# Gate and up stage of an encoder: who casts, who sums and who empties PSUM

## The chip, the core and the metric

One core of one Trainium2 chip runs the whole kernel in one launch. TensorE (PE; PEld is its weight load) multiplies, VectorE (DVE), ScalarE (ACT) and GpSimd (POOL) do the rest, and SyncE (SP) issues the DMAs. The metric is the device time of one execution in microseconds; lower is better. Three runs of the kernel before took 3045.6 to 3051.87 us, median 3049.84.

## The reference, cut to what matters

Two encoder layers over 1024 tokens of width 1024, in float32. Each layer has a mixer (attention), a layer norm, a gated feed-forward with a convolution of width 3 over the tokens, another layer norm, and a gated addition of an embedding. The change lies in the first half of the feed-forward, in both layers:

```python
def conv_ffn(x, w_gate, w_up, conv_w, conv_b, w_down):   # x 1024x1024, w_gate and w_up 1024x2816
    a = x @ w_gate
    u = x @ w_up
    ap = jnp.pad(a, ((0, 0), (pad, pad), (0, 0)))
    c = conv_b
    for j in range(CONV_WIDTH):
        c = c + conv_w[j] * ap[:, j:j + S]
    return (jax.nn.gelu(c) * u) @ w_down
```

## The kernel before

**How the work is staged.** A layer runs as projections and attention, output projection and layer norm, the gate and up stage, the down projection, and the embedding. The gate and up stage takes x transposed, with the even and the odd tokens apart, and cuts `w_gate` and `w_up` into 22 pieces (`NF`), gate and up by turns: piece m holds two blocks of 128 output columns. Each piece is one matrix product of 2 x 2 blocks, done by the Strassen-Winograd scheme with seven block products in place of eight. The weights' sides of the seven are `a00`, `a01`, `a11` (blocks as loaded) and the sums `s1` to `s4`; the sides of x are `b00`, `b10`, `b11` and `t1` to `t4`, made once in the layer (in the trace `xb` and `xt`).

**Float32 by three matmuls.** TensorE multiplies values of a shorter format (float32r). So each operand is split: a cast gives its high part, a subtraction on VectorE the low part (`lo_part`, line 142), and `mm3` (lines 159 to 161) issues high x high, high x low and low x high. A block product is 4 x 3 = 12 matmuls of 512 columns, added up in one PSUM bank.

**The helpers that the change touches.** `Weights.sums` makes `s1` to `s4`: with an engine given, `s1`'s first addition and `s3` run there and the other two on VectorE (`ws` in the trace, line 319). `Weights.split` casts one side and subtracts: for the names in `HI` (`s3`, `a01`, `a11`) the cast is GpSimd's (`pool_copy`, line 139), for the other four ScalarE's (line 325). `Weights.steps` lists the sums and the seven splits of a piece.

`Products.read` empties PSUM and adds the products up to the four result blocks, as far as they are there: `m` is ScalarE's copy of the product `a00`; `u2 = m + s2`, `u3 = u2 + s3` and so on are additions on VectorE with one operand in PSUM (`plus`, line 1332). The products `a00` and `s2` of a piece share one tile of two banks (`pa`, two such tiles); the other five rotate through four banks (`pb`). The first two pieces go ahead (`go_ahead`): their products come in another order, `s1` before `s2`, with an extra copy of `s1` (`k5`) that two additions then use (lines 1353 and 1354).

**What sets the order.** The tile framework puts each engine's instructions into a fixed order when the program is built, by its own estimate of when each can run, and adds the waits; on the chip an engine works through its order and stops at a wait. The list `order` in `ffn` gives the products: the first two pieces interleaved, then seven products for each of the rest. The third piece's preparation (`todo`) is spread over the first two pieces' last products, and each later piece's over the products of the one before.

Of the kernel before, what the change touches and what calls it, by code (L numbers as in the profile page):

```python
# [12 lines left out]
ALU = mybir.AluOpType  # L13
# [19 lines left out]
def tile_hybrid_encoder(  # L33
# [32 lines left out]
    nc = tc.nc  # L66
# [12 lines left out]
    def unit(s, shape, dt=F32):  # L79
        return up.tile(shape, dt, tag="u", name=nm(s))  # L80
# [26 lines left out]
    def rtile(s, shape, dt=F32R):  # L107
        return region[0].tile(s, shape, dt)
# [7 lines left out]
    def mid2(s, shape, dt=F32):  # L116
        return sm.tile(shape, dt, tag="mid2", name=nm(s), bufs=4)
# [10 lines left out]
    def f32(ap):  # L128
        return ap.bitcast(F32)
# [8 lines left out]
    def pool_copy(o, i):  # L138
        nc.gpsimd.tensor_scalar(o, i, 1.0, 1.0, op0=ALU.mult, op1=ALU.mult)  # L139

    def lo_part(lo, src, hi):
        nc.vector.tensor_tensor(lo, src, f32(hi), op=ALU.subtract)  # L142

    def split(raw, h, l, hi=None, lo=None):
        if hi is nc.scalar:
            nc.scalar.copy(h, raw)  # L146
        else:
            pool_copy(h, raw)
        (lo or nc.vector).tensor_tensor(l, raw, f32(h), op=ALU.subtract)  # L149

    def load_split(dram, shape, s, make=runit, hi=None, lo=None):
        r = region[0].raw(s + "r", shape)
        nc.sync.dma_start(out=r, in_=dram)
        h, l = make(s + "h", shape), make(s + "l", shape)
        split(r, h, l, hi, lo)
        return h, l
# [161 lines left out]
    def add(o, a, b, op=ALU.add, eng=None):  # L318
        return (eng or nc.vector).tensor_tensor(f32(o), f32(a), f32(b), op=op)

    def split_value(v, h, l, hi=None):
        if hi is nc.gpsimd:
            pool_copy(h, v)
        else:
            nc.scalar.copy(h, v)  # L325
        lo_part(l, v, h)
# [316 lines left out]
    class BlockB:  # L643
# [7 lines left out]
        def steps(self):  # L651
            out = []
            if self.pr % 2 == 0:
                out += [self.g.load] + [lambda t=t: self.g.project(t) for t in range(NT)]
            out.append(self.load)
            out += [lambda t=t: self.project(t) for t in range(NT)]
            return out
# [249 lines left out]
    class MixTiles:  # L907
# [4 lines left out]
        def seven(self, t):  # L912

            mr = region[0].raw("mr", [P, NK, P])
            nc.sync.dma_start(out=mr[:, 0:7, :], in_=mix[self.i].rearrange("k p q -> p k q")[:, 0:7, t * P:(t + 1) * P])
            two = [runit("mhl", [P, 2, 4, P]) for _ in range(2)]
            for j, m in enumerate(two):
                n = 4 - j
                split(mr[:, 4 * j:4 * j + n], m[:, 0, 0:n], m[:, 1, 0:n])
            self.m[t] = mr, two  # L920
# [342 lines left out]
    class Weights:  # L1263
# [22 lines left out]
            for step in steps:  # L1286
                step()

        HI = {"s3", "a01", "a11"}

        def split(self, name, raw=None):
            raw = name in ("a00", "a01") if raw is None else raw
            hl = region[0].raw("w", [P, 2, 4, P], F32R) if raw else rtile("w", [P, 2, 4, P])
            self.h[name], self.l[name] = hl[:, 0], hl[:, 1]
            split_value(self.v[name], hl[:, 0], hl[:, 1], nc.gpsimd if name in self.HI else None)

        def steps(self):

            return [lambda: self.sums(nc.gpsimd)] + [lambda n=n: self.split(n) for n in Products.ORDER]

    class Products:

# [26 lines left out]
        def read(self):  # L1329

            def plus(o, a, name):
                nc.vector.tensor_tensor(o, a, self.o[name], op=ALU.add)  # L1332
            out = []
            had = set(x for x, _ in self.sums)
            for name, need in list(self.sums):
                before = {"m": (), "u2": ("m",), "u3": ("u2",), "c11": ("u3",), "c00": ("m",) if self.ahead else ("u2",), "c10": ("u3", "c11"), "k5": (),
                          "c01": ("c11",)}[name]
                if any(x not in self.o for x in need) or any(x in had for x in before):
                    continue
                if name == "m":  # L1340
                    self.m = mid2("m", [P, 512])
                    nc.scalar.copy(self.m, self.o["a00"])
                elif name == "u2":
                    u = unit("u", [P, 2, 512])
                    self.u2, self.u3 = u[:, 0, :], u[:, 1, :]
                    plus(self.u2, self.m, "s2")
                elif name == "u3":
                    plus(self.u3, self.u2, "s3")
                elif name == "k5":
                    self.c11 = mid2("c11", [P, 512])  # L1350
                    nc.scalar.copy(self.c11, self.o["s1"])
                elif name == "c11" and self.ahead:
                    nc.gpsimd.tensor_tensor(self.u2, self.u2, self.c11, op=ALU.add)
                    nc.vector.tensor_tensor(self.c11, self.u3, self.c11, op=ALU.add)
                elif name == "c11":
                    self.c11 = mid2("c11", [P, 512])
                    plus(self.c11, self.u3, "s1")
                    plus(self.u2, self.u2, "s1")
                elif name == "c00":
                    if self.c00 is None:  # L1360
                        self.c00 = self.m
                    plus(self.c00, self.m, "a01")
                elif name == "c10":
                    plus(self.u3, self.u3, "a11")
                    self.c10 = self.u3
                elif name == "c01":
                    plus(self.u2, self.u2, "s4")
                    self.c01 = self.u2
                had.discard(name)
                out.append(name)  # L1370
            self.sums = [x for x in self.sums if x[0] in had]
            return out
# [14 lines left out]
    def ffn(i, w, xt, late, prefetch):  # L1387
# [3 lines left out]
        def new_c():  # L1391
            late_c.append(big("c", [P, 2, 1024]))
# [51 lines left out]
        def finished(n):  # L1444
            if n >= 0:
                m = order[n][0]
                for name in pr[m].read():
                    use(pr[m], m, name)
# [12 lines left out]
        todo = []  # L1461
        for n, (m, name) in enumerate(order):
            finished(n - 1)
            pr[m].product(name)
            if n == 0:
                c00 = unit("c00", [P, 2, 512])
                for a in range(2):
                    pr[a].go_ahead(c00[:, a])
                for a in range(2):
                    sums[a] = w[a].sums()  # L1470
                    sums[a][0]()
                    w[a].split("s1")
            if n == 1:
                late()
                new_c()
                temps = [late_c[0][:, a, :].rearrange("p (k q) -> p k q", k=2) for a in range(2)]
            if n == 2:
                for a in range(2):
                    sums[a][1]()
                    sums[a][2]()  # L1480
                    w[a].split("s4")
            if n == 3:
                for a in range(2):
                    xt.finish("t2", a)
                for a in range(2):
                    w[a].split("s2", True)
            if n == 4:
                for a in range(2):
                    xt.finish("t3", a)
                for a in range(2):  # L1490
                    sums[a][3]()
                    w[a].split("s3")
            if n == 5:
                for a in range(2):
                    xt.finish("t4", a, temps[a])
            if n == 6:
                w[0].split("a11")
                w[1].split("a11")
                w[2].load()
            if n == 7:  # L1500
                w[3].load()
                todo = w[2].steps()
            for _ in range({8: 1, 10: 2, 11: 1, 12: 1, 13: 3}.get(n, 0)):
                todo.pop(0)()
            if m >= 2 and m + 1 < NF:
                j = Products.ORDER.index(name)
                if j == 0:
                    todo = w[m + 1].steps()
                    todo[0]()
                    if m + 2 < NF:  # L1510
                        w[m + 2].load()
                todo[j + 1]()
            if m == NF - 1:
                down.ahead(Products.ORDER.index(name))
# [98 lines left out]
    for i in range(2):  # L1613
        if i == 0:
            w, mt, oT = mixer_ab(xt)
        else:
            tc.keep_in_program_order(nc.scalar.preload_act_table_set("natural_log_exp_and_others"))
            w, mt, oT = mixer_c(xt, late)
# [107 lines left out]
```

## Time and profile before

| | us |
|---|---|
| median of three runs | 3049.84 |
| the profiled execution | 3047.42 |
| its span in the trace | 3045.1 |
| TensorE busy | 2949.2 (97%) |
| VectorE busy | 2308.2 (76%) |
| ScalarE busy | 1318.1 (43%) |
| GpSimd busy | 963.6 (32%) |

The first layer's gate and up stage lies between about 795 and 1240 us of the span, the second layer's between about 2285 and 2730. A timeline row gives the start, the duration, engine and line, what is written from what, and in brackets how long the engine had been idle and what ended that. `xN` on a row means N equal instructions in a row, whose duration is that of all. In a row of windows the granted clock is TensorE's, as a share of full speed.

### The profile page before, as it was taken

The page shows a single profiled execution, that of the slowest core. Times are in us where ns is not written, and L with a number is a line of the kernel's source. Part 1 is how long each engine was busy: PE and PEld are TensorE (multiplying, and loading weights), DVE is VectorE, ACT ScalarE, POOL GpSimd, SP SyncE. Part 2 cuts the span into 40 slices and gives each one's busy share as a digit, 9 for nine tenths or more (in the row PEclk, how much of TensorE's full clock was granted, in tenths as well). Part 3 has the DMA queues.
Part 4 walks back from the last instruction along what each step waited for, and adds up shares of the span by engine and source line. Part 5 has one row for each costly group of instructions (what it writes and reads, how often), then busy time and mean ns, then how long its engine had stood idle before and what let it go on. Part 6 is the DMA issues. An engine that isn't in the chain of part 4 may idle for free.

```text
span 3045.1 us, 42940 instructions
## 1 busy us (share of the span) xinstructions
PE 2949.2 (97%) x15456; PEld 2533.8 (83%) x15456; DVE 2308.2 (76%) x4022; ACT 1318.1 (43%) x2806; POOL 963.6 (32%) x1484
## 2 busy tenths in 40 slices
PE   8999999999989999999999999999998999999999
PEld 7888989887768888888888999998776788888887
DVE  6666477876898888688648777777769888877874
ACT  4555477761222222345225555555413222234431
POOL 4444544243232222000225555554332222210012
PEclk9999999999999999999999999999999999999999
DMA  3000100034223332734111100001431333346331
GB/s 123 29 28 19 38 29 8 8 130 134 90 98 104 104 104 100 276 133 169 63 59 34 34 32 29 28 18 56 155 129 69 115 104 104 104 163 244 115 127 66
DMA packets 119715, 272.10 MB, mean 89 GB/s; under 512 B 11344, under 2 KB 35024, under 8 KB 119504
## 3 DMA queue, kind: packets, MB, share of 16 engines
q1 hardware_dynamic: 119504, 269.37, 26.0%
q8 instruction: 122, 2.00, 0.3%
q14 instruction: 89, 0.73, 0.1%
HBM read 196.46 MB, written 72.88 MB: 88 GB/s over the span
## 4 chain that ended last, share of the span: by engine, by line
PE 74%; DVE 15%; ACT 3%; issue 3%; POOL 3%; DMA 2%; SPq 0%; DVEq 0%; ACTq 0%; POOLq 0%
PE pb L159 5%; PE pb L161 5%; PE pb L160 5%; PE xt L164 5%; PE pp L159 4%; PE s L588 4%; PE pp L161 4%; PE pp L160 4%; PE pd L159 4%; PE pd L161 4%; PE pd L160 4%; PE pa L159 2%; PE pg L159 2%; PE pg L161 2%; PE pg L160 2%
## 5 line engine op out<-in xcount | busy, mean ns | idle before, releaser
L142 DVE TENSOR_TENSOR ptl<-xt,pth 128x512 fp32r<-128x512 f32 (+2 forms) x384 | 239.7, 652 | 60.2 <-ACT pth L399 43.6
L159 PE MATMUL pp<-wh,xth 128*128 128x384 f32 x768 | 266.1, 347 | 8.0 <-ACT wh L146 7.6
L160 PE MATMUL pp<-wl,xth 128*128 128x384 f32 x768 | 258.8, 337 | 2.0 <-DVE wl L149 1.8
L161 PE MATMUL pp<-wh,xtl 128*128 128x384 f32 x768 | 257.9, 336 | 0.0
L440 ACT ACTIVATE e<-s,nmx 128x1024 f32<-128x1024 f32 x192 | 214.7, 1120 | 81.7 <-DVE nmx L838 59.0
L160 PE MATMUL pd<-wd,gd 128*128 128x512 f32 x616 | 239.9, 389 | 0.2 <-DVE wd L142 0.2
L159 PE MATMUL pd<-wd,gd 128*128 128x512 f32 x616 | 239.8, 389 | 0.0
L161 PE MATMUL pd<-wd,gd 128*128 128x512 f32 x616 | 239.7, 389 | 0.0
L325 ACT CAST w<-ws 128x512 fp32r<-128x512 f32 x132 | 81.1, 621 | 336.6 <-PE pb L161 281.0
L164 PE MATMUL xt<-ident,e 128*128 128x128 f32 x1440 | 198.1, 274 | 9.6 <-POOL e L740 3.0
L159 PE MATMUL pb<-xt,w 128*128 128x512 f32 x528 | 207.1, 392 | 0.0
L160 PE MATMUL pb<-xt,w 128*128 128x512 f32 x528 | 206.9, 392 | 0.0
L161 PE MATMUL pb<-xt,w 128*128 128x512 f32 x528 | 206.6, 391 | 0.0
L1149 ACT CAST gd<-gr 128x512 fp32r<-128x512 f32 x154 | 96.0, 623 | 214.9 <-PE pd L161 176.1
L164 PEld LDWEIGHTS xt<-ident,e 128*128 128x128 f32 x1440 | 163.5, 141 | 30.4 <-ACT sq L870 5.9
L896 POOL TENSOR_SCALAR rs<-mv 128x1 f32<-128x1 f32 x32 | 9.3, 291 | 547.7 <-DVE mv L895 547.1
L139 POOL TENSOR_SCALAR w<-ws 128x512 fp32r<-128x512 f32 x44 | 33.4, 760 | 467.0 <-PE pa L161 416.8
L142 DVE TENSOR_TENSOR gd<-gr,gd 128x512 fp32r<-128x512 f32 x154 | 106.1, 689 | 77.1 <-ACT gd L1149 77.1
L142 DVE TENSOR_TENSOR w<-ws,w 128x512 fp32r<-128x512 f32 x176 | 152.4, 870 | 5.2 <-ACT w L325 3.1
L159 PEld LDWEIGHTS pp<-wh,xth 128*128 128x128 f32 x768 | 144.6, 188 | 13.3 <-ACT wh L146 8.2
L838 DVE TENSOR_REDUCE nmx<-s 128x1 f32<-128x1024 f32 x128 | 150.4, 1214 | 2.6 <-PE s L588 2.6
L159 PE MATMUL pb<-xb,w 128*128 128x512 f32 x352 | 139.9, 397 | 9.8 <-DVE u L1332 5.7
(292 smaller groups left out, 8905.2 us busy)
## 6 DMA issues: line engine op xcount, KB each, us to landing
gr<-gated SPq DMA_DIRECT2D x76, 512.0 KB, 3.7
gated<-c SPq DMA_DIRECT2D x90, 256.0 KB, 3.5
wf<-in_w_gate_dram SPq DMA_DIRECT2D x44, 512.0 KB, 4.1
wf<-in_w_up_dram SPq DMA_DIRECT2D x44, 512.0 KB, 4.2
wd<-in_w_down_dram SPq DMA_DIRECT2D x44, 512.0 KB, 5.5
wr<-in_w_c_dram SPq DMA_DIRECT2D x32, 384.0 KB, 3.3
gated<-u SPq DMA_DIRECT2D x44, 256.0 KB, 2.2
pes<-peo SPq DMA_DIRECT2D x64, 128.0 KB, 1.9
```

The costliest lines, as they stand in the source:

```text
L139: nc.gpsimd.tensor_scalar(o, i, 1.0, 1.0, op0=ALU.mult, op1=ALU.mult)
L142: nc.vector.tensor_tensor(lo, src, f32(hi), op=ALU.subtract)
L159: nc.tensor.matmul(o, lhsT=lh, rhs=rh, start=start, stop=False)
L160: nc.tensor.matmul(o, lhsT=lh, rhs=rl, start=False, stop=False)
L161: nc.tensor.matmul(o, lhsT=ll, rhs=rh, start=False, stop=stop)
L164: nc.tensor.transpose(o, in_=i, identity=ident)
L325: nc.scalar.copy(h, v)
L440: nc.scalar.activation(dst, s, AF.Exp, bias=negmax, scale=1.0, accum_out=l)
L588: nc.tensor.matmul(s[:, kh * 512:kh * 512 + 512], lhsT=qt[:, hl, i, :], rhs=self.ks[kh][:, j, :], start=hl == 0, stop=hl == 1)
L838: nc.vector.tensor_reduce(out=nmx, in_=s, axis=AX.X, op=ALU.max, negate=True)
L896: nc.gpsimd.tensor_scalar(rs, mv[:, 1:2], 1.0, LN_EPS, op0=ALU.mult, op1=ALU.add)
L1149: nc.scalar.copy(g[:, 0], rg)
```

## The change

In the gate and up stage of both layers: the casts of `s3`, `a01` and `a11` go from GpSimd to ScalarE, as those of the other four sides; the sums of the third and fourth piece run on VectorE alone (those of the first two did already; from the fifth piece on GpSimd keeps its two); the first two pieces' `s2` is copied out of PSUM by ScalarE, and an addition of two SBUF operands on VectorE adds `m`; and the addition of `u2` and `c11` in these two pieces goes from GpSimd to VectorE.

```diff
--- before.py
+++ after.py
@@ -1286,17 +1286,15 @@
             for step in steps:
                 step()
 
-        HI = {"s3", "a01", "a11"}
-
         def split(self, name, raw=None):
             raw = name in ("a00", "a01") if raw is None else raw
             hl = region[0].raw("w", [P, 2, 4, P], F32R) if raw else rtile("w", [P, 2, 4, P])
             self.h[name], self.l[name] = hl[:, 0], hl[:, 1]
-            split_value(self.v[name], hl[:, 0], hl[:, 1], nc.gpsimd if name in self.HI else None)
-
-        def steps(self):
-
-            return [lambda: self.sums(nc.gpsimd)] + [lambda n=n: self.split(n) for n in Products.ORDER]
+            split_value(self.v[name], hl[:, 0], hl[:, 1])
+
+        def steps(self, eng):
+
+            return [lambda: self.sums(eng)] + [lambda n=n: self.split(n) for n in Products.ORDER]
 
     class Products:
 
@@ -1343,14 +1341,18 @@
                 elif name == "u2":
                     u = unit("u", [P, 2, 512])
                     self.u2, self.u3 = u[:, 0, :], u[:, 1, :]
-                    plus(self.u2, self.m, "s2")
+                    if self.ahead:
+                        nc.scalar.copy(self.u2, self.o["s2"])
+                        add(self.u2, self.u2, self.m)
+                    else:
+                        plus(self.u2, self.m, "s2")
                 elif name == "u3":
                     plus(self.u3, self.u2, "s3")
                 elif name == "k5":
                     self.c11 = mid2("c11", [P, 512])
                     nc.scalar.copy(self.c11, self.o["s1"])
                 elif name == "c11" and self.ahead:
-                    nc.gpsimd.tensor_tensor(self.u2, self.u2, self.c11, op=ALU.add)
+                    nc.vector.tensor_tensor(self.u2, self.u2, self.c11, op=ALU.add)
                     nc.vector.tensor_tensor(self.c11, self.u3, self.c11, op=ALU.add)
                 elif name == "c11":
                     self.c11 = mid2("c11", [P, 512])
@@ -1499,13 +1501,13 @@
                 w[2].load()
             if n == 7:
                 w[3].load()
-                todo = w[2].steps()
+                todo = w[2].steps(nc.vector)
             for _ in range({8: 1, 10: 2, 11: 1, 12: 1, 13: 3}.get(n, 0)):
                 todo.pop(0)()
             if m >= 2 and m + 1 < NF:
                 j = Products.ORDER.index(name)
                 if j == 0:
-                    todo = w[m + 1].steps()
+                    todo = w[m + 1].steps(nc.vector if m == 2 else nc.gpsimd)
                     todo[0]()
                     if m + 2 < NF:
                         w[m + 2].load()
```

What this makes of the order, at the place where the first two pieces end and the third begins. ScalarE, first layer; `xt4` is the last side of x, `w_2516`, `w_2523`, `w_2517`, `w_2519`, `w_2521`, `w_2524`, `w_2525` are the third piece's `a00`, `a01`, `s2`, `s3`, `s1`, `a11`, `s4`; `pa_2463` and `pa_2478` hold the first two pieces' `a00` and `s2`. Before:

```order
L325 CAST xt4_2498_10540<-c_2477_10441 128x1024
L1399 ACTIVATE c_2477_10441<-c00_2464_10384,convt_81 128x512
L325 CAST xt4_2500_10546<-c_2477_10441 128x1024
L325 CAST w_2516_10641<-wf_2506_10573 128x512
L325 CAST w_2517_10644<-ws_2511_10606 128x512
L325 CAST w_2521_10694<-ws_2511_10606 128x512
L1399 ACTIVATE c_2477_10441<-c11_2496_10525,convt_81 128x512
L1399 ACTIVATE c_2477_10441<-u_2513_10612,convt_81 128x512
L325 CAST w_2525_10724<-ws_2512_10607 128x512
```

After:

```order
L325 CAST xt4_2498_10540<-c_2477_10441 128x1024
L1401 ACTIVATE c_2477_10441<-c00_2464_10384,convt_81 128x512
L325 CAST xt4_2500_10546<-c_2477_10441 128x1024
L325 CAST w_2516_10643<-wf_2506_10573 128x512
L325 CAST w_2523_10720<-wf_2506_10573 128x512
L325 CAST w_2517_10646<-ws_2511_10606 128x512
L1345 COPY u_2513_10612<-pa_2463_10371 128x512
L1345 COPY u_2514_10627<-pa_2478_10443 128x512
L325 CAST w_2519_10673<-ws_2512_10607 128x512
L325 CAST w_2521_10696<-ws_2511_10606 128x512
```

The casts of `a01` and `s3` have come over from GpSimd, and the two copies out of `pa` stand behind the cast of the third piece's `s2` (`w_2517`).

VectorE at the same place; `ws_2511` and `ws_2512` hold the third piece's sums, `u_2513` and `u_2514` the first two pieces' `u2` and `u3`. Before:

```order
L142 TENSOR_TENSOR xt4_2501_10547<-c_2477_10441,xt4_2500_10546 128x1024
L142 TENSOR_TENSOR w_2523_10718<-wf_2506_10573,w_2523_10718 128x512
L142 TENSOR_TENSOR w_2516_10641<-wf_2506_10573,w_2516_10641 128x512
L319 TENSOR_TENSOR ws_2511_10606<-ws_2511_10606,wf_2506_10573 128x512
L319 TENSOR_TENSOR ws_2512_10607<-wf_2506_10573,ws_2511_10606 128x512
L1332 TENSOR_TENSOR u_2513_10612<-m_2471_10397,pa_2463_10371 128x512
L1332 TENSOR_TENSOR u_2514_10626<-m_2481_10466,pa_2478_10443 128x512
L142 TENSOR_TENSOR w_2517_10644<-ws_2511_10606,w_2517_10644 128x512
L1332 TENSOR_TENSOR u_2513_10612<-u_2513_10612,pb_2515_10628 128x512
L142 TENSOR_TENSOR w_2519_10671<-ws_2512_10607,w_2519_10671 128x512
L1332 TENSOR_TENSOR u_2514_10626<-u_2514_10626,pb_2518_10658 128x512
```

After:

```order
L142 TENSOR_TENSOR xt4_2501_10547<-c_2477_10441,xt4_2500_10546 128x1024
L142 TENSOR_TENSOR w_2516_10643<-wf_2506_10573,w_2516_10643 128x512
L142 TENSOR_TENSOR w_2523_10720<-wf_2506_10573,w_2523_10720 128x512
L319 TENSOR_TENSOR ws_2511_10606<-wf_2507_10574 128x512
L319 TENSOR_TENSOR ws_2512_10607<-wf_2506_10573,wf_2507_10574 128x512
L319 TENSOR_TENSOR ws_2511_10606<-ws_2511_10606,wf_2506_10573 128x512
L319 TENSOR_TENSOR ws_2512_10607<-wf_2506_10573,ws_2511_10606 128x512
L142 TENSOR_TENSOR w_2517_10646<-ws_2511_10606,w_2517_10646 128x512
L319 TENSOR_TENSOR u_2513_10612<-u_2513_10612,m_2471_10397 128x512
L319 TENSOR_TENSOR u_2514_10627<-u_2514_10627,m_2481_10466 128x512
L1330 TENSOR_TENSOR u_2513_10612<-u_2513_10612,pb_2515_10630 128x512
L142 TENSOR_TENSOR w_2519_10673<-ws_2512_10607,w_2519_10673 128x512
```

The two additions that read `pa` (line 1332) are gone; two more sums of the third piece have come in ahead of the place where they stood, and two additions of SBUF operands (line 319) behind it. Further on, TensorE's order has ten matmuls of the fourth piece's `a00` ahead of the third piece's last product where it had four, and GpSimd's has nothing between the layer norms' small operations and the fifth piece's sums. From the fifth piece on TensorE's order is as before.

## Rows read from the trace of the kernel before

**Rows 1.** The page's busy time, share of the span and instructions by engine.

```profile
PE 2949.2 (97%) x15456; PEld 2533.8 (83%) x15456; DVE 2308.2 (76%) x4022; ACT 1318.1 (43%) x2806; POOL 963.6 (32%) x1484
```

**Rows 2.** Busy us by stretch, layer one's stage: PE, PEld, DVE, ACT, POOL, clock, DMA.

```profile
830.00:870.00 40.00, 30.76 (x123) 24.64 (x123) 38.78 (x45) 11.88 (x15) 20.28 (x15) 0.87 0.22 73
870.00:890.00 20.00, 17.14 (x68) 13.42 (x68) 19.27 (x30) 8.37 (x13) 5.11 (x4) 0.91 0.43 158
890.00:1210.00 320.00, 318.80 (x1394) 259.96 (x1393) 278.18 (x403) 90.00 (x131) 87.15 (x84) 1.00 0.30 101
```

**Rows 3.** TensorE's waits, 785 to 1215: line, cause, us in total, times, longest.

```profile
PE pa L159 <- DVE u L1332: 9.2, 1, 9.2
PE pb L159 <- DVE u L1332: 2.9, 1, 2.9
PE pa L159 <- ACT m L1342: 1.2, 3, 0.5
```

**Rows 4.** TensorE's timeline: start, us, line, out and in, count, idle before and releaser.

```profile
838.66 0.39 PE L161 MATMUL pb<-xt,w 128*128 128x512 f32 x1
...
848.29 0.77 PE L159 MATMUL pa<-xb,w 128*128 128x512 f32 x1 [9.24 <-DVE u L1332]
...
854.06 0.47 PE L159 MATMUL pb<-xt,w 128*128 128x512 f32 x1
...
873.67 0.39 PE L159 MATMUL pa<-xb,w 128*128 128x512 f32 x1
...
876.91 0.50 PE L159 MATMUL pb<-xb,w 128*128 128x512 f32 x1 [2.86 <-DVE u L1332]
...
881.23 0.53 PE L160 MATMUL pa<-xb,w 128*128 128x512 f32 x1
...
2333.57 0.77 PE L159 MATMUL pa<-xb,w 128*128 128x512 f32 x1 [9.24 <-DVE u L1332]
```

**Rows 5.** TensorE after the first gap: busy us, granted clock, DMA.

```profile
848.00:854.00 6.00, 5.71 (x13) 0.50 0.01 3
```

**Rows 6.** VectorE's timeline before the first gap's end.

```profile
830.45 1.22 DVE L319 TENSOR_TENSOR c<-xb,t 128x1024 f32<-128x1024 f32 x1
832.18 2.12 DVE L142 TENSOR_TENSOR w<-ws,w 128x512 fp32r<-128x512 f32 x2 [0.51 <-POOL w L139]
...
847.46 1.28 DVE L1332 TENSOR_TENSOR u<-m,pa 128x512 f32<-128x512 f32 x2
```

**Rows 7.** VectorE's groups, 790 to 1240: busy us, mean ns of one, idle before.

```profile
L319 DVE TENSOR_TENSOR c<-c,xb 128x1024 f32<-128x1024 f32 x2 | 3.9, 1956 | 0.0
...
L142 DVE TENSOR_TENSOR xt<-c,xt 128x1024 fp32r<-128x1024 f32 x2 | 3.8, 1882 | 0.1
```

**Rows 8.** GpSimd's timeline, its first and last work around the first gap.

```profile
830.12 2.62 POOL L139 TENSOR_SCALAR w<-ws 128x512 fp32r<-128x512 f32 x2 [25.03 <-DVE ws L319]
...
842.89 1.05 POOL L139 TENSOR_SCALAR w<-wf 128x512 fp32r<-128x512 f32 x1
```

**Rows 9.** Tiles `pb` (whole run), `ws` (790 to 1240): count, ns min/median/max, starts.

```profile
L1332 DVE TENSOR_TENSOR u<-u,pb x172: 672/678/689, 849.3 to 2732.1; 128x512 f32<-128x512 f32 x172
...
L142 DVE TENSOR_TENSOR w<-ws,w x88: 675/687/1780, 801.9 to 1226.2; 128x512 fp32r<-128x512 f32 x88
```

**Rows 10.** ScalarE's largest group of casts, 790 to 1240.

```profile
L325 ACT CAST w<-ws 128x512 fp32r<-128x512 f32 x66 | 40.6, 620 | 167.5 <-PE pb L161 139.7 <-DVE c L1407 16.7 <-DVE ws L319 10.4
```

**Rows 11.** ScalarE's timeline before the first gap.

```profile
824.15 0.58 ACT L1351 COPY c<-pb 128x512 f32<-128x512 f32 x1
...
835.94 1.05 ACT L325 CAST xt<-c 128x1024 fp32r<-128x1024 f32 x1 [9.31 <-DVE c L319]
```

**Rows 12.** VectorE's timeline between the two gaps.

```profile
848.65 0.69 DVE L142 TENSOR_TENSOR w<-ws,w 128x512 fp32r<-128x512 f32 x1
...
851.71 1.75 DVE L1354 TENSOR_TENSOR c<-u,c 128x512 f32<-128x512 f32 x1 [0.57 <-POOL u L1353]
...
876.19 0.67 DVE L1332 TENSOR_TENSOR u<-u,pb 128x512 f32<-128x512 f32 x1
```

## The prediction

> **What bounds the kernel now.** I began with the busy times of the page [rows 1]: TensorE is busy for 97% of the span, VectorE for 76%, ScalarE for 43%, GpSimd for 32%. So only time in which TensorE stands still, or runs its matmuls slowly, can be won. The busy times by stretch [rows 2] say where that is in the first layer's gate and up stage: in the 320 us of the regular pieces (890 to 1210) TensorE is idle for 1.2 us, in the 40 us before 870 for 9.2 us, and in the 20 us after that for 2.9 us.
>
> TensorE's waits [rows 3] name the reason: one wait of 9.2 us and one of 2.9 us, both for VectorE's line 1332, which adds a product out of PSUM; and three waits, 1.2 us together, for ScalarE's copy of `m`. The matmuls beside the two long waits [rows 4] give their price. The last one before the first gap starts at 838.66, the next at 848.29; a regular matmul takes 318.8 / 1394 = 0.23 us [rows 2], so 9.63 - 0.23 = 9.4 us are lost. Then thirteen matmuls take 5.77 us, from 848.29 to 854.06, where 13 x 0.23 = 3.0 would do: another 2.8 us. The granted clock was 0.50 in 848 to 854 [rows 5] against 1.00 in the regular pieces, the lower of the two levels (1.2 GHz in place of 2.4). The second gap loses 876.91 - 873.67 - 0.23 = 3.0 us, and the twelve matmuls up to 881.23 lose 4.32 - 12 x 0.23 = 1.6 us. Layer two repeats this (its first gap is the last of [rows 4], 9.24 us again), so every term counts twice.
>
> **What the first gap waits for.** TensorE wants the PSUM banks that hold the first and second product of the first piece (`pa`), for the first product of the third. VectorE frees them with its add at 847.46, last of a queue of which [rows 6, 7] show the pieces that matter. In that queue equal operations have unequal lengths: 1.22 us for the 1024 columns at 830.45, but 1.96 and 1.88 in the mean for the four operations of that size in two later groups; 1.28 us for two of 512 columns at 847.46, but 2.12 for the two at 832.18. The long ones lie where GpSimd works, from 830.12 to 842.89 + 1.05 [rows 8]. Line 1332, with one operand in PSUM, takes 672 to 689 ns in all of its 172 runs on `u`, while the subtraction of SBUF operands at line 142 reaches 1780 ns [rows 9].
>
> **The change part by part.**
>
> *Casts to ScalarE.* Per layer 66 casts leave GpSimd (three for each of 22 pieces) and cost ScalarE 66 x 0.62 = 41 us, by the 66 that it has of this size [rows 10]. ScalarE is busy for 90 of the 320 regular us [rows 2]; some 50 more casts there add 31 us, and it stays under 40%. I cost them at nothing; their cover is ScalarE's idle time, and where it fails the first rival below applies.
>
> In the first pieces they act on VectorE. ScalarE is idle from 826.63 to 835.94 [rows 11], so the four casts that VectorE waits for (two of `s3`, two of `a11`) run there from 830 and are done by 830 + 4 x 0.62 = 832.5. VectorE's queue then is, in starts (two operations of 512 columns take 1.28 us, each of them 0.68, so they overlap by 0.08 and occupy 0.60 and, with 1024 columns, 1.14): `c` 830.45; two subtractions 831.6 and 832.2; two of 1024 at 832.8 and 833.9; `w` 835.1; `xt` 835.7; `c` 836.8; `w` 837.95. The last `xt` needs ScalarE's cast of `c`, which starts when `c` ends at 838.0 and takes 1.05 [rows 11]: 839.2. Then two subtractions at 840.35 and 840.95.
>
> *Sums of the third and fourth piece on VectorE.* Four more additions per layer on VectorE, two of them here: 841.55 and 842.15. The sum `s2` follows at 842.75 and ends at 843.4.
>
> *The second product copied by ScalarE.* The copy itself needs nothing later than 833; but ScalarE's order puts it behind the cast of the third piece's `s2`, and that needs the sum of 843.4. So the cast runs 843.45 to 844.05, the copy of 0.58 us (as the other copies out of PSUM, [rows 11]) to 844.55, and TensorE starts at 844.7, the same 0.15 us behind as in [rows 4]. The gap shrinks by 848.3 - 844.7 = 3.6 us; it does not close. From below this is bounded by the long operations staying long: 2 x (1.96 - 1.22) + 2 x (1.88 - 1.22) + (2.12 - 1.28) = 3.6 us, with which nothing would be won. From above, by a copy that waited for no sum, when TensorE could start with its subtracted weights at 841: 7 us. I take 3.6, the length at 830.45, since GpSimd then has no work in this stretch. For the slow matmuls after it I take no gain (bounds 0 and 1.2 us, the difference of 2.8 and 1.6).
>
> *Additions in place of GpSimd's.* VectorE gets two `u` plus `c11` additions and two sums of the fourth piece before the read that frees the bank of the second gap. In the order before, 38 instructions lead from 848.65 to the end of that read at 876.86, 28.2 us [rows 12]; 38 x 0.60 would be 22.8. The excess of 5.4 us holds a wait for GpSimd and an operation of 1.75 us beside it at 851.71; I allow 0.5 of it for eight three-operand instructions, which are a little longer, and put the rest to GpSimd. After, 41 instructions run from 844.7: 41 x 0.60 + 0.5 = 25.1, and with 0.5 us allowed for casts that come late, they end at 870.3. TensorE, 25.6 us of work after its restart (848.29 to 873.67 + 0.23), with six more matmuls ahead by its new order (1.4 us) and 0.2 us for a bank, arrives at 844.7 + 27.2 = 871.9. So it no longer waits: 3.0 + 1.6 = 4.6 us. Lower bound 0 (VectorE stays 3 us later than I count), upper bound 4.6.
>
> By the Trainium skill ("SBUF — State Buffer", Who interferes with whom) a VectorE instruction with two SBUF inputs contends with a GpSimd instruction that reads SBUF, and one with at most one SBUF input does not. That speaks against this part: the `u` sum, of the kind that was never late in [rows 9], becomes one of two SBUF inputs. By the rule it could take as long as the 1.78 us of line 142. I count nothing for it: GpSimd's next work in the new order is the fifth piece's sums, behind the read that matters here.
>
> *The rest.* Ahead of the stage two of GpSimd's casts become ScalarE's, beside the last output projection; nothing. The order of the DMA queue's stores changes with VectorE's; TensorE waits for none of them. The three waits of 1.2 us stay.
>
> **Sum.** Per layer 3.6 + 4.6 - 0.2 = 8.0 us, twice 16. The profiled execution took 3047.4 us (span 3045.1), so 3031.4; the median of the runs shown is 3049.84, 2.4 us above, which gives 3033.8. I predict 3033.
>
> **Rivals.**
>
> *ScalarE gets late in the regular pieces (slower).* TensorE's second product of a piece waits for ScalarE's copy of `m`, in whose front stands a cast that starts only when the first product ends: 0.62 + 0.58 us, less the overlap, against six or seven matmuls (1.4 to 1.6 us at 0.23 each) of cover. For it: the three short waits in [rows 3], and every other copy has a gelu and an activation before that cast. If one more cast of 0.6 us stands before each of the 36 copies, 36 x 0.6 = 21.6 us go, and 16 come: 3049.8 + 5.6 = 3055. It decides from 0.45 us a piece. Against it: in the new order the same kinds of instruction stand right ahead of each copy as before.
>
> *The first gap stays.* If the long operations are not GpSimd's doing, the copy behind the sum comes no sooner, and VectorE, with eight more additions a layer, 4.8 us, frees the second gap's bank no sooner either: between 3050 and 3041 (with the second gap alone closed). Against it: the times of [rows 8] beside those of [rows 6].
>
> *The second gap stays.* VectorE is busy for 38.8 of the 40 us to 870 [rows 2], and my margin is 1.6 us. Then only 2 x 3.4 = 6.8 us: 3043.
>
> *More.* If the copy goes ahead of that sum or the shorter gap leaves the clock alone, up to 7.0 + 2.8 + 4.6 = 14.4 per layer: 3021.
>
> **How the numbers follow.** Forecast 0.67; second gap stays 0.10; first gap stays 0.10; ScalarE late 0.07; more 0.06. A change of under 0.2% (6 us) can't be told from none by these measurements. Faster: 0.67 + 0.06 + half of the second-gap case (0.05) and a little of the first-gap case (0.03) = 0.81. Slower: 0.07. The rest, 0.12, is no change. The range 3025 to 3044 leaves out the slower case, most of the first-gap case, and half of the gains beyond 12 us per layer, about 0.2.
>
> **What would show it.** In the profile after: VectorE's operations of 1024 columns at 1.22 us throughout the stretch after the third products; TensorE's wait before the third piece's first product at some 5.7 us and ended by ScalarE's copy at line 1345; no wait before the last product of the third piece; regular pieces as before, TensorE idle for under 2 us in 320. A wait for the copy of `m` in most pieces, or 1.6 us operations on VectorE with GpSimd silent, would make the prediction wrong.

## The result, and the profile after

The changed kernel takes 3031.25 us (median of 4 runs, 3026.32 to 3034.22), the kernel before 3049.27 us (4 runs, 3045.60 to 3051.87). The ratio is 0.9938, 95% interval 0.9926 to 0.9951: faster by 18 us, where 16 were forecast. The profiled execution of the changed kernel took 3034.22 us, with a span of 3032.4. One of the eleven executions of the run `no_casts` below took 14057 us and is left out of its ratio.

The page's busy time by engine, beside [rows 1]: ScalarE has 82 us more, GpSimd 111 us less, TensorE the same work.

```profile
PE 2949.4 (97%) x15456; PEld 2537.1 (84%) x15456; DVE 2287.9 (75%) x4034; ACT 1400.2 (46%) x2942; POOL 853.0 (28%) x1340
```

The busy times by stretch, which answer to [rows 2] (PE, PEld, DVE, ACT, POOL, clock, DMA share, GB/s):

```profile
830.00:870.00 40.00, 34.49 (x145) 27.65 (x145) 39.45 (x59) 18.51 (x28) 0.00 (x0) 0.96 0.29 103
870.00:890.00 20.00, 20.00 (x90) 16.47 (x89) 20.00 (x30) 10.40 (x17) 8.77 (x4) 1.00 0.26 96
890.00:1210.00 320.00, 317.70 (x1383) 259.07 (x1382) 274.48 (x404) 120.53 (x180) 52.55 (x33) 0.99 0.30 104
```

GpSimd does nothing from 830 to 870, and TensorE idles there for 5.5 us in place of 9.2. From 870 to 890 it does not idle at all. But in the regular pieces it now idles for 2.3 us in place of 1.2, and that is new. TensorE's waits in the two layers' stages (785 to 1215, then 2270 to 2720), beside [rows 3], name it:

```profile
PE pa L159 <- ACT u L1345: 5.5, 1, 5.5
PE pa L159 <- ACT m L1340: 2.3, 1, 2.3
...
PE pa L159 <- ACT m L1340: 1.4, 1, 1.4
```

The first gap is ended by ScalarE's copy (L1345, the same length in both layers), the second gap is gone, and in place of three short waits for the copy of `m` there is one long one: 2.3 us in layer one, 1.4 us in layer two. It stands before the second product of the sixth piece (the expectations further down miscount it as the seventh or eighth). TensorE's timeline around the gaps, beside [rows 4] (start, us, line, out and in, idle before and releaser):

```profile
841.15 0.39 PE L161 MATMUL pb<-xt,w 128*128 128x512 f32 x1
847.04 0.79 PE L159 MATMUL pa<-xb,w 128*128 128x512 f32 x1 [5.51 <-ACT u L1345]
...
850.41 0.39 PE L159 MATMUL pb<-xt,w 128*128 128x512 f32 x1
...
915.73 0.39 PE L159 MATMUL pb<-xt,w 128*128 128x512 f32 x1
918.42 0.72 PE L159 MATMUL pa<-xt,w 128*128 128x512 f32 x1 [2.30 <-ACT m L1340]
...
921.92 0.41 PE L161 MATMUL pa<-xt,w 128*128 128x512 f32 x1
```

So the first gap costs 847.04 - 841.15 - 0.23 = 5.7 us, and the seven matmuls after it 3.37 - 7 x 0.23 = 1.8 us (before: 9.4 and 2.8). In layer two, behind a wait of the same length, thirteen matmuls are slow, from 2325.40 to 2331.44: 6.04 - 13 x 0.23 = 3.1 us, where before's twelve cost 2.6:

```profile
2325.40 0.79 PE L159 MATMUL pa<-xb,w 128*128 128x512 f32 x1 [5.51 <-ACT u L1345]
```

The new wait costs 918.42 - 915.73 - 0.23 = 2.5 us, and its eight slow matmuls 3.5 - 8 x 0.23 = 1.7. (Layer one's times lie some 2.5 us later than before's: this execution came later into the stage. The run `sums_all`, with the same code up to this gap, came to it 2.2 us earlier than before, so the offset is none of the change's doing.)

VectorE's timeline, beside [rows 6], first in front of the first gap's end, then the read that frees the second gap's bank:

```profile
832.94 1.22 DVE L319 TENSOR_TENSOR c<-xb,t 128x1024 f32<-128x1024 f32 x1
834.07 1.28 DVE L142 TENSOR_TENSOR w<-ws,w 128x512 fp32r<-128x512 f32 x2
835.28 1.21 DVE L319 TENSOR_TENSOR c<-c,xb 128x1024 f32<-128x1024 f32 x1
...
841.62 1.23 DVE L142 TENSOR_TENSOR xt<-c,xt 128x1024 fp32r<-128x1024 f32 x1 [0.51 <-ACT xt L325]
842.76 1.29 DVE L142 TENSOR_TENSOR w<-wf,w 128x512 fp32r<-128x512 f32 x2
...
845.17 0.68 DVE L319 TENSOR_TENSOR ws<-ws,wf 128x512 f32<-128x512 f32 x1
...
871.70 0.68 DVE L1330 TENSOR_TENSOR u<-u,pb 128x512 f32<-128x512 f32 x1
```

All operations of 1024 columns take 1.21 to 1.23 us, and the pair of `w` 1.28 in place of 2.12. ScalarE in the same stretch, beside [rows 11]: the casts that VectorE used to wait for, then the cast that waits 3.27 us for VectorE's sum, and both copies behind it:

```profile
832.45 1.23 ACT L325 CAST w<-ws 128x512 fp32r<-128x512 f32 x2 [3.33 <-DVE ws L319]
833.58 1.14 ACT L325 CAST w<-wf 128x512 fp32r<-128x512 f32 x2
...
845.88 0.62 ACT L325 CAST w<-ws 128x512 fp32r<-128x512 f32 x1 [3.27 <-DVE ws L319]
846.41 1.07 ACT L1345 COPY u<-pa 128x512 f32<-128x512 f32 x2
```

The new wait is followed back in a row of GpSimd, a row of VectorE, and two of ScalarE (a gelu, and the copy of `m` behind it, with an activation and a cast between them, as in the kernel before):

```profile
906.14 1.60 POOL L319 TENSOR_TENSOR ws<-wf 128x512 f32<-128x512 f32 x1 [15.91 <-DVE u L1330]
```

```profile
907.77 1.76 DVE L319 TENSOR_TENSOR ws<-ws,wf 128x512 f32<-128x512 f32 x1 [1.19 <-POOL ws L319]
```

```profile
915.62 1.06 ACT L1405 ACTIVATE c<-c 128x1024 f32<-128x1024 f32 x1 [2.17 <-DVE c L1403]
...
917.80 0.57 ACT L1340 COPY m<-pa 128x512 f32<-128x512 f32 x1
```

GpSimd's sum `s1` for the seventh piece starts only when VectorE has read a `u` for the last time (a buffer of that pool comes free). VectorE then stands 1.19 us for that sum, and its own `s2` takes 1.76 us beside GpSimd's `s3` instead of 0.68. The adds and the gate behind it come late, so does ScalarE's gelu, and the copy of `m` stands behind that gelu on ScalarE. That reading was first an inference; the run `sums_all` below tests the sums' part in it, and `casts_only` shows that they are not all of it.

### The profile page after: what moved, and what is told of

Same layout as the page of the kernel before. It is cut to its first block, busy times and chain, and to the rows that moved or that the text cites. A ratio compares the mean times of both kernels' runs of the same rounds, so it can differ in the third digit from the quotient of the medians.

```text
span 3032.4 us, 42892 instructions
## 1 busy us (share of the span) xinstructions
PE 2949.4 (97%) x15456; PEld 2537.1 (84%) x15456; DVE 2287.9 (75%) x4034; ACT 1400.2 (46%) x2942; POOL 853.0 (28%) x1340
## 4 chain that ended last, share of the span: by engine, by line
PE 77%; DVE 13%; ACT 3%; issue 2%; POOL 2%; DMA 2%; SPq 0%; DVEq 0%; ACTq 0%; POOLq 0%
PE pb L159 6%; PE pb L160 6%; PE pb L161 6%; PE xt L164 5%; PE pp L159 4%; PE pp L160 4%; PE pp L161 4%; PE pd L161 4%; PE pd L159 4%; PE pd L160 4%; PE s L588 3%; PE pa L159 2%; PE pa L161 2%; PE pa L160 2%; PE pg L159 2%
## 5 line engine op out<-in xcount | busy, mean ns | idle before, releaser
L319 POOL TENSOR_TENSOR ws<-wf 128x512 f32<-128x512 f32 x36 | 64.5, 1793 | 563.8 <-DMA gated<-u 200.2
L325 ACT CAST w<-ws 128x512 fp32r<-128x512 f32 x176 | 107.9, 621 | 214.6 <-PE pb L161 127.6
L325 ACT CAST w<-wf 128x512 fp32r<-128x512 f32 x132 | 80.8, 619 | 179.9 <-PE pb L161 123.6
L160 PEld LDWEIGHTS pp<-wl,xth 128*128 128x128 f32 x768 | 145.3, 189 | 4.9 <-DVE wl L149 4.7
```

What stands on the lines that cost most here:

```text
L160: nc.tensor.matmul(o, lhsT=lh, rhs=rl, start=False, stop=False)
```

## Experiments

The two theories at the start. A: the casts on GpSimd lengthened VectorE's operations; with the casts gone VectorE's queue is shorter, and the copy by ScalarE is worth nothing since it stands behind the sum `s2`. B: the copy freed the bank early, or the moved sums did. Each run was executed five times, `no_casts` eleven times; ratios are to the kernel before, run on the same chip.

**no_copy: the change without ScalarE's copy.**

```
 elif name == "u2":
-    if self.ahead:
-        nc.scalar.copy(self.u2, self.o["s2"])
-        add(self.u2, self.u2, self.m)
-    else:
-        plus(self.u2, self.m, "s2")
+    plus(self.u2, self.m, "s2")
```

> The change without its third part: VectorE again reads the second product out of PSUM itself and adds m in the same instruction. Theory A (the first gap shrank because GpSimd is silent beside VectorE; the copy stands behind the sum s2 anyway and gives next to nothing): VectorE's two adds come right behind the four sums, 1.2 us after them, so the first gap's wait is 5.5 to 6.3 us and ended by VectorE, the second gap stays closed, and the time is that of the change or up to 2 us more, 3030 to 3034, ratio to before 0.993 to 0.995. Rival B (the copy by ScalarE is what freed the bank early): the wait goes back to about 9 us, 7 us over both layers are lost, 3038, ratio 0.9965.

Measured 3031.05 us, ratio 0.9938 (0.9925 to 0.9952), the same as the change. TensorE's waits, first layer one, then layer two:

```profile
PE pa L159 <- DVE u L1330: 5.7, 1, 5.7
PE pa L159 <- ACT m L1340: 2.1, 1, 2.1
...
PE pa L159 <- DVE u L1330: 5.8, 1, 5.8
...
PE pa L159 <- ACT m L1340: 1.6, 1, 1.6
```

The copy buys 0.2 to 0.3 us of the first gap. Theory B falls for the copy.

**casts_only: the kernel before, with only the casts moved.**

```
-        HI = {"s3", "a01", "a11"}
+        HI = set()
```

> The kernel before with the casts alone moved to ScalarE; GpSimd keeps the sums of the third and fourth piece and the two u plus c11 additions, VectorE reads the second product. Theory A: the four casts beside 830 to 836 no longer lengthen VectorE's operations, but the two sums on GpSimd (3.9 us before) still lengthen two operations of 1024 columns by about 1 us each, while VectorE has two sums (1.2 us) fewer in front of the add: first gap 6 to 7.5 us, second gap 0 to 2 us, time 3036 to 3042, ratio 0.9955 to 0.9975. Rival B (copy and moved sums bring the gain): both gaps stay at 9.2 and 2.9 us, ratio 1.000.

Measured 3031.30 us, ratio 0.9943 (0.9930 to 0.9955): the casts alone bring what the whole change brings, within the intervals. TensorE's waits are as theory A has them (6.1 us, and 1.7 us at the second gap, in both layers). The time is better than I expected, in part since the wait for the copy of `m` is absent in both layers: TensorE is busy for all 310 us from 890 to 1200 (columns as above):

```profile
890.00:1200.00 310.00, 310.00 (x1357) 253.19 (x1356) 270.15 (x394) 118.82 (x177) 50.41 (x33) 1.00 0.31 103
```

Yet GpSimd's sum for the seventh piece is late here too: VectorE stands 1.18 us for it, and its own sum at 905.44 takes 1.77 us, as in the change. TensorE is only 5.9 us ahead of before at that place, where the change's is 9.7 us ahead; it starts that product at 917.92 without a wait, just behind ScalarE's copy, which ends at 917.87. VectorE's timeline, then GpSimd's, in front of the first gap's end:

```profile
836.17 1.22 DVE L142 TENSOR_TENSOR xt<-c,xt 128x1024 fp32r<-128x1024 f32 x1
...
839.64 1.71 DVE L142 TENSOR_TENSOR xt<-c,xt 128x1024 fp32r<-128x1024 f32 x1 [0.52 <-ACT xt L325]
841.27 2.35 DVE L142 TENSOR_TENSOR w<-wf,w 128x512 fp32r<-128x512 f32 x2
```

```profile
837.26 3.00 POOL L319 TENSOR_TENSOR ws<-wf 128x512 f32<-128x512 f32 x1 [31.63 <-DMA wf<-in_w_gate_dram]
840.23 2.24 POOL L319 TENSOR_TENSOR ws<-wf,wf 128x512 f32<-128x512 f32 x1
```

The same line 142 takes 1.22 us before GpSimd gets going and 1.71 beside it; the later pair of `w` takes 2.35 us, against 1.29 in the change, where GpSimd is silent.

**no_casts: the change with the casts of `s3`, `a01` and `a11` back on GpSimd.**

```
+        HI = {"s3", "a01", "a11"}
...
-            split_value(self.v[name], hl[:, 0], hl[:, 1])
+            split_value(self.v[name], hl[:, 0], hl[:, 1], nc.gpsimd if name in self.HI else None)
```

> The change with the casts of s3, a01 and a11 back on GpSimd; sums on VectorE and copy on ScalarE as in the change. Theory A: GpSimd works from 830 to 843 as before, VectorE's operations of 1024 columns are 1.6 to 2.3 us long again and it has four sums in front of the copy: the first gap's wait is 8.5 to 10.5 us, ended by ScalarE's copy that waits for a VectorE sum; the second gap stays mostly closed (0 to 2 us); time 3038 to 3046, ratio 0.9965 to 0.999. Rival B: wait of 5.5 us, as in the change, ratio 0.994.

Measured 3046.33 us, ratio 0.9984 (0.9975 to 0.9993): some three quarters of the gain are gone. The casts beside VectorE lengthen its operations again (GpSimd from 831 to 837, then VectorE):

```profile
831.02 2.62 POOL L139 TENSOR_SCALAR w<-ws 128x512 fp32r<-128x512 f32 x2 [25.03 <-DVE ws L319]
833.60 3.62 POOL L139 TENSOR_SCALAR w<-wf 128x512 fp32r<-128x512 f32 x3
```

```profile
833.09 2.10 DVE L142 TENSOR_TENSOR w<-ws,w 128x512 fp32r<-128x512 f32 x2 [0.52 <-POOL w L139]
835.11 1.62 DVE L319 TENSOR_TENSOR c<-c,xb 128x1024 f32<-128x1024 f32 x1
836.66 1.63 DVE L319 TENSOR_TENSOR c<-xb,t 128x1024 f32<-128x1024 f32 x1
...
839.95 1.21 DVE L319 TENSOR_TENSOR c<-c,xb 128x1024 f32<-128x1024 f32 x1
```

The first gap's wait is 7.7 us, under the 8.5 to 10.5 that I expected: past 837, where GpSimd has run out of casts and the sums are not its own, VectorE is back at 1.21 us. Of the 2.2 us by which the wait exceeds the change's, the three long rows hold 1.6 (0.82, 0.41 and 0.41), and VectorE's wait for GpSimd's cast 0.5. What the time lacks is elsewhere, in waits for the copy of `m`, 5.4 us in layer one and 3.6 in layer two. The longest, again before the sixth piece's second product, in TensorE's timeline:

```profile
922.18 0.79 PE L159 MATMUL pa<-xt,w 128*128 128x512 f32 x1 [4.14 <-ACT m L1342]
```

So with the casts on GpSimd the sixth piece costs more as well as the first gap; by which step they do it there was not followed.

**no_sums: the change with the sums of the third and fourth piece back on GpSimd.**

```
-                todo = w[2].steps(nc.vector)
+                todo = w[2].steps(nc.gpsimd)
...
-                    todo = w[m + 1].steps(nc.vector if m == 2 else nc.gpsimd)
+                    todo = w[m + 1].steps(nc.gpsimd)
```

> The change with the sums s1 and s3 of the third and fourth piece back on GpSimd; casts and copy on ScalarE, u plus c11 on VectorE as in the change. Theory A: two VectorE operations of 1024 columns are lengthened by about 1 us each by the two sums beside them, and VectorE saves two sums of 0.6 us: the first gap is 5 to 7 us; near the second gap the fourth piece's sums lengthen some VectorE operations by up to 1 us each, its bank comes 0 to 2 us late; time 3030 to 3037, ratio 0.9935 to 0.996. Rival C (GpSimd beside VectorE costs nothing, the lengths come from elsewhere): first gap 4.3 us, time 3028 or less.

Measured 3033.56 us, ratio 0.9948 (0.9936 to 0.9961), not told apart from the change. The first gap's wait is 5.8 us: VectorE's two sums fewer (1.2 us) are paid back by longer operations beside GpSimd's two (1.71 for 1.22, and 2.35 for 1.28). The second gap is 0.6 us in layer one and 0.2 in layer two. The copy of `m` costs 1.1 in each, here before the fifth piece's second product. Of rival C's 4.3 us there is nothing.

After these, the gain's cause stood, and the 2.3 and 1.4 us at the sixth piece were open. Theory D: the late GpSimd sum causes them. Theory E: VectorE's queue as such is full, and TensorE, now earlier, runs into it. More sums on VectorE would help by D and hurt by E.

**sums_all: the change, with the sums of all later pieces on VectorE.**

```
-                    todo = w[m + 1].steps(nc.vector if m == 2 else nc.gpsimd)
+                    todo = w[m + 1].steps(nc.vector)
```

> The change, with the sums s1 and s3 of all later pieces on VectorE too, so that GpSimd has no work in the stage. It asks where the new wait of 2.3 us for the copy of m (seventh piece, layer one; 1.4 us in layer two) comes from. Theory D (a GpSimd sum that starts late holds VectorE up): VectorE never waits for GpSimd and none of its operations is lengthened, the wait and the slow matmuls after it go: 3024 to 3028, ratio 0.992 to 0.993. Theory E (VectorE's queue, busy without a break from 830 to 890, is itself the limit of the first seven pieces, and TensorE, which comes earlier than before, runs into it): two more sums of 0.6 us a piece make the wait longer, 3 to 6 us per layer, and it may come again: 3034 to 3042, ratio 0.995 to 0.998.

Measured 3026.73 us, ratio 0.9923 (0.9911 to 0.9936), on theory D's side. No wait for the copy of `m` is left in either layer; of the stage's waits for a `u` or an `m` only the first gap's stays (5.5 us). The regular pieces by stretch, layer one and two (columns as above):

```profile
920.00:1200.00 280.00, 280.00 (x1226) 228.62 (x1224) 239.99 (x384) 106.86 (x159) 0.00 (x0) 1.00 0.30 102
2366.00:2680.00 314.00, 314.00 (x1373) 256.16 (x1373) 270.20 (x431) 121.02 (x181) 0.00 (x0) 1.00 0.31 106
```

TensorE is busy throughout. And VectorE pays nearly nothing for the additions. Its groups of `ws<-wf,ws` and `ws<-ws,wf` (890 to 1200) in the change, where GpSimd adds beside them (count, busy us, mean ns, idle before):

```profile
L319 DVE TENSOR_TENSOR ws<-wf,ws 128x512 f32<-128x512 f32 x17 | 19.6, 1150 | 0.6
...
L319 DVE TENSOR_TENSOR ws<-ws,wf 128x512 f32<-128x512 f32 x17 | 12.7, 747 | 6.4 <-POOL ws L319 6.4
```

and in `sums_all`:

```profile
L319 DVE TENSOR_TENSOR ws<-wf,wf 128x512 f32<-128x512 f32 x17 | 11.6, 684 | 0.0
...
L319 DVE TENSOR_TENSOR ws<-wf,ws 128x512 f32<-128x512 f32 x17 | 11.6, 684 | 0.0
...
L319 DVE TENSOR_TENSOR ws<-ws,wf 128x512 f32<-128x512 f32 x17 | 11.6, 683 | 0.0
```

The change's row for layer two:

```profile
2366.00:2680.00 314.00, 312.60 (x1368) 255.25 (x1367) 271.85 (x399) 119.61 (x179) 55.37 (x34) 1.00 0.30 103
```

In this stretch VectorE runs 32 instructions more in `sums_all` (431 against 399) and is busy for 1.7 us less (270.20 against 271.85). The sums taken from GpSimd cost 0.68 us each; GpSimd beside them had cost VectorE about as much.

**pinned: TensorE's order around the first gap altered.** The `u` tiles are taken ahead of the third piece's load, and ScalarE's cast of that piece's `a00` is kept behind what stands ahead of it in the program; the scheduler then puts TensorE's 24 matmuls first.

```
+                for a in range(2):
+                    pr[a].u = unit("u", [P, 2, 512])
...
+            cast = nc.scalar.copy(h, v)
+            if pin:
+                tc.keep_in_program_order(cast)
```

> The change with the order around the first gap altered: TensorE runs the 24 matmuls of the first two pieces on the fourth sum of the tokens (5.5 us) ahead of the third piece's first product, and ScalarE's copies of the second products stand earlier. Theory E (VectorE is the limit of the first seven pieces): the first gap shrinks from 5.5 to 0 to 3 us, but TensorE gives most of it back in waits for VectorE's adds and for the copy of m before the eighth piece: 3027 to 3033, ratio 0.9925 to 0.9945. Rival F (the first gap is a loss by itself): 3 to 5.5 us per layer and the slow matmuls stay won: 3018 to 3025, ratio 0.990 to 0.992.

Measured 3028.95 us, ratio 0.9933 (0.9921 to 0.9946). Neither theory was tested, since the gap did not shrink. TensorE's first matmul behind it:

```profile
846.84 0.77 PE L159 MATMUL pb<-xt,w 128*128 128x512 f32 x1 [6.44 <-DVE u L1332]
```

The 24 matmuls that I wanted as cover need a bank `pb`, and that bank is freed by VectorE's add of the third product, which stands behind the same sums. Both kinds of bank come free through the same queue. This run has no wait for the copy of `m` in layer one and 0.2 us in layer two; its GpSimd sum at 904.10 waits for the weights' DMA and not for a `u`. It is 1.30 us long, and VectorE does not wait for it.

**pinned_no_sums: that, with the third and fourth piece's sums on GpSimd** (the edit of `no_sums`).

> As the run named pinned, and the sums s1 and s3 of the third and fourth piece on GpSimd, which takes four additions of 0.6 us a layer from VectorE. Theory E: what VectorE is spared up to the eighth piece, 2.4 us less some 2 us by which GpSimd's sums lengthen two or three of its operations, comes back at TensorE: the same as pinned or up to 2 us a layer less, 3025 to 3032. Theory D: GpSimd's sums hold VectorE up once more, waits grow by 1 to 2 us a layer: 3030 to 3036.

Measured 3030.81 us, ratio 0.9943 (0.9930 to 0.9957); the first gap's wait is 6.8 us, the copy of `m` costs 0.5 and 1.3. For the same reason as above it tells the theories no further apart.

**sums_all_no_copy: the best version without the copy** (the edits of `sums_all` and `no_copy`).

> The run named sums_all without ScalarE's copy of the second product: VectorE reads it out of PSUM itself, so two instructions a layer fewer on ScalarE and none more on VectorE. If the copy is worth nothing because it stands behind the sum s2 (as in the run no_copy), first gap 5.7 us ended by VectorE, no other wait in the stage, 3024 to 3029, ratio 0.992 to 0.993, and this is the simpler of the two best versions. If the copy matters once GpSimd's sums are gone, a wait of 1 to 3 us a layer appears at the second gap or at the copy of m: 3029 to 3033.

Measured 3027.49 us, ratio 0.9924 (0.9911 to 0.9938), first gap 5.8 and 5.7 us ended by VectorE, no other wait for a `u` or an `m`. It and `sums_all` are the best kernels here, some 4 us under the change by their medians; the intervals of the three ratios overlap.

## Why the prediction was right

*What the first gap waits for, and its size.* Right. VectorE's queue shortened because GpSimd was silent, the operations of 1024 columns went to 1.22 us, the copy ran behind the cast that waits for `s2`, and the wait was 5.51 us where 5.7 were forecast. The gap's cost fell from 9.4 to 5.7: 3.7 us, forecast 3.6. `no_casts` and `casts_only` show that it was mainly the casts: moved alone they take 3.1 us off the wait (9.2 to 6.1), put back they add 2.2 (5.5 to 7.7).

*Slow matmuls after it, taken at nothing with bounds 0 and 1.2.* Not the same in both layers: in layer one 2.8 became 1.8, a gain of 1.0 us; in layer two 2.6 became 3.1, a loss of 0.5.

*The second gap.* Right in the change: both layers lose it, with the 4.6 us that were forecast for it. VectorE's read ends at 871.70 + 0.68 = 872.4, which is 869.9 on before's time line (2.5 us earlier); 870.3 was forecast. TensorE comes for the bank at 872.89, so the margin was 0.5 us, where I had 1.6, and it was needed: with GpSimd's sums in it the gap is 0.6 us (`no_sums`), with GpSimd's `u` additions too, and without the copy, 1.7 us (`casts_only`). No run puts the `u` plus `c11` additions back alone.

*The copy by ScalarE.* Right that it does not close the gap; what it is worth I had not separated. It is 0.2 to 0.3 us (`no_copy`).

*Casts on ScalarE at nothing.* Right: ScalarE is busy for 120.5 of 320 us (38%), with casts of 0.62 us as in [rows 10].

*"The three short waits of 1.2 us stay."* Wrong, and the one step with a mechanism missed. They went, and a single wait took their place that costs 2.5 + 1.7 = 4.2 us in layer one. Matched matmul by matmul (each layer's stage has 1848 in both traces), and counted from the last one ahead of the first gap, TensorE's lead over before is 9.7 us by then in layer one and 8.4 in layer two; it falls there by 4.1 and 1.5, and grows again by 1.8 and 0.9 up to the stage's end, as before's short waits fall away. I had looked only at GpSimd near the two gaps, and had costed what stays of it in the regular pieces as before. A TensorE that comes 9.7 us earlier meets a sum on GpSimd that is late. `sums_all` shows that without GpSimd's sums the wait goes; `casts_only`, which has the same late sum and a lead of 5.9 us but no wait, shows that the sum alone does not make it. That the release of a buffer makes the sum late is read from the trace and was not tried by itself.

*The sum.* By that matching a layer gains 7.5 and 7.8 us up to the stage's end, where 8.0 were forecast. The terms, in the order first gap, slow matmuls behind it, second gap, the new wait, the rest of the stage, are 3.73 + 1.12 + 4.83 - 4.05 + 1.84 = 7.47 for layer one and 3.73 - 0.33 + 4.96 - 1.47 + 0.92 = 7.81 for layer two. (The second gap's term is here over the forecast's 4.6, and the slow matmuls' not quite as above, since a few matmuls past the ones counted are slow too.) So that the total came so near is partly luck: gains that were not foreseen (1.8 and 0.9 us, and in layer one another 1.1) stood against a loss that was not foreseen (4.1 and 1.5). The medians differ by 18.0 us, 2.7 more than the two stages' 15.3; the profiled execution is the slowest of its four, and differs from before's by 13.2.

*A count.* The rival of the first gap reckons with eight more additions a layer on VectorE. They are six, four sums and two `u` plus `c11`: VectorE's instructions went from 4022 to 4034 over both layers.

*The Trainium skill's rule.* VectorE's additions with one operand in PSUM were never late: 672, 680 and 689 ns (shortest, median, longest of the 172 at line 1330), while the subtraction `w<-ws,w` reaches 1804. The sums that now have two SBUF operands, and which I costed without delay, were not late either, with GpSimd silent beside them: `u` plus `c11` took 680 to 683 ns in all four of its runs, and the pair of `u` plus `m` at 847.14 took 1.28 us. In the two stages of all ten profiles (790 to 1240 and 2290 to 2735 us), VectorE's sums and subtractions of two SBUF operands took at most 0.70 us for 512 columns and 1.23 for 1024 where no GpSimd instruction ran beside them, and up to 1.83 and 2.31 where one did; those with an operand in PSUM stayed at 0.69 beside GpSimd too. By the Trainium skill ("SBUF — State Buffer", Who interferes with whom) a VectorE instruction with two SBUF inputs contends with a GpSimd instruction that reads SBUF. The trace agrees: the longer ones stand only where GpSimd runs.

## What to carry to other kernels

Where VectorE is the busy engine, work that GpSimd does on SBUF beside it is not free: look for operations of equal size and unequal length, and add up the excess before crediting GpSimd with relief. A copy that frees a bank early is worth only as much as its place on its engine's queue allows. And when a gap shrinks, follow the engine that now comes earlier to the next place with a thin margin: here 4.1 of the 9.7 us that layer one had won were taken back 45 us later.

## What the hardware showed beyond that

GpSimd suffers too. Its sum of 128x512, in the change 1.28 us at the shortest, took 4.70 us once in each layer, beside a dense stretch of VectorE whose own sums took 0.68 us:

```profile
883.55 4.70 POOL L319 TENSOR_TENSOR ws<-wf 128x512 f32<-128x512 f32 x1 [7.11 <-DVE c L1403]
```

And the length of a wait does not by itself tell how many slow matmuls follow. In the change eight follow the wait of 2.3 us (behind 918.42); the wait of 5.5 us is followed by seven in layer one (behind 847.04) and by thirteen in layer two (behind 2325.40); layer two's wait of 1.4 us by none. The granted clock was 0.73 and 0.76 of full speed in the mean of the stretches around the first gap and the new wait in layer one, and 0.50, the lower of the two levels, throughout the one behind layer two's first gap (columns as above):

```profile
847.00:853.00 6.00, 5.96 (x19) 4.38 (x20) 6.00 (x11) 3.56 (x7) 0.00 (x0) 0.73 0.01 3
915.00:922.00 7.00, 4.70 (x14) 3.42 (x14) 6.19 (x8) 3.81 (x5) 1.68 (x1) 0.76 0.00 0
2325.00:2331.00 6.00, 5.60 (x12) 3.97 (x13) 6.00 (x11) 3.56 (x7) 0.00 (x0) 0.50 0.00 0
```
